# Row means of a 64 MB tensor: the first rows in parts of their own, and the last rows summed as two halves at once

## The chip, the cores and the metric

The kernel runs on one core of a Trainium2 chip. The metric is the device time of one execution in microseconds. Before the change it is 161.2 us, the median of 8 runs (161.05 to 161.87).

## The reference

```python
x = np.random.randn(32, 512, 1024).astype(np.float32)
divisor = 1024.0

def reference(x, divisor):
    return (np.sum(x, axis=-1) / divisor).astype(np.float32)
```

There are 32 x 512 = 16384 rows of 1024 floats (4 KB each, 67.1 MB in all). Each row is summed and multiplied by 1/1024. The output is 16384 floats, 64 KB.

## The kernel before

The 16384 rows are spread over the 128 partitions, 128 rows to each. They are cut into two parts in memory. The main part has M = 112 rows per partition: partition p holds rows 112p to 112p + 111, so that two neighbouring partitions read addresses 448 KB apart. The last part has L = 16 rows per partition, 64 KB apart, behind the main part.

The main part is loaded as tiles of 2, 14 (six times), 14 and 12 rows per partition, into a pool `bulk` of three buffers of 14 rows. The last part is loaded as 8, 4 and 2 rows, one whole row (`row`), and one row in three pieces of 448, 256 and 320 columns (`pa`, `pb`, `pc`). The 8-row tile takes a buffer of `bulk`; the rest have tiles of their own in the pool `one`. All loads are issued by SP in program order (line 142), and the loads of one core run through the same 16 DMA engines in that order. A load into a `bulk` buffer waits until DVE is done with the tile that was in it.

DVE sums rows with `reduce_sum` (line 153), all rows of a tile in one instruction. For the later tiles ACT takes some of the rows, one instruction for each row, which writes a copy to PSUM that nobody reads and the sum as its accumulator (line 147): 4 of 14, 5 of 12, 4 of 8, 2 of 4, 1 of 2. The sums of the main part go to `res`, which GpSimd scales once, after the last of them (line 189), and which SP then stores (line 190). The sums of the last part go to `q`. Of the whole row, DVE sums 768 columns into `q` (line 176) and ACT sums and scales 256 into `r`. At the end ACT sums `pa` and DVE sums `pb` (line 193), each into a spare column of `pc`; DVE makes `fin` from `q` and `r` (line 194), and then scales `pc` with its two spare columns and sums it, in one instruction with an accumulator (line 198), into the last column of `fin`. SP stores `fin` (line 201).

Three functions rearrange the finished program, and the change leaves them as they are. The first loads, which wait for nothing, are moved ahead of the start barrier. The waits of an instruction are sorted, so that the one expected last stands last. The last store is moved behind SP's waits for every other transfer and engine, and the closing barriers run while it is in flight; its own wait, for DVE, is kept on it. So SP issues the last store only after all earlier loads and stores have landed.

Of the kernel before, what the change touches and what calls it, by code (L numbers as in the profile page):

```python
# [8 lines left out]

F32 = mybir.dt.float32  # L10
ADD = mybir.AluOpType.add
MULT = mybir.AluOpType.mult
COPY = mybir.ActivationFunctionType.Copy
AX = mybir.AxisListType.X
SP = mybir.EngineType.SP
# [52 lines left out]
def close_while_storing(nc, landed):  # L68


    body, end = nc.main_func.blocks[1], nc.main_func.blocks[-1]
    store = [i for i in body.instructions if i.engine == SP and type(i).__name__ == "InstDMACopy"][-1]
    (lane,) = store.sync_info.on_update
    drain = end.instructions[0]
    assert drain.engine == SP and type(drain).__name__ == "InstDrain"
    needs = {w.id: w for w in drain.sync_info.on_wait}
    assert needs[lane.id].wait_value > lane.update_value
    needs[lane.id] = dataclasses.replace(
        needs[lane.id], wait_value=needs[lane.id].wait_value - lane.update_value
    )  # L80

    (done,) = [w for w in store.sync_info.on_wait if w.ant_name.startswith("DVE_")]
    assert needs[done.id].wait_value == done.wait_value
    del needs[done.id]
    own = dict(sync_type="semaphore", id=landed.num, ant_name=landed.name)
    add = mybir.SyncUpdate(update_mode="sem-add-imm", update_value=16, **own)
    sub = mybir.SyncUpdate(update_mode="sem-sub-imm", update_value=16, **own)
    last = nc.sync.wait_ge(landed, 16).ins
    assert nc.main_func.blocks[-1].instructions[-1].name == last.name
    body.instructions = [i for i in body.instructions if i.name != store.name]  # L90
    end.instructions = [
        with_sync(drain, on_wait=tuple(needs.values())),
        with_sync(store, on_wait=(done,), on_update=(add,)),
        *end.instructions[1:-1],
        with_sync(last, on_update=(sub,)),
    ]


@with_exitstack
def kernel(  # L100
    ctx: ExitStack,
    tc: tile.TileContext,
    x: bass.AP,
    divisor: float,
    out: bass.AP,
):
    nc = tc.nc
    landed = nc.alloc_semaphore("landed")
    nc.at_finalize(start_loads_at_once)
    nc.at_finalize(latest_wait_first)  # L110
    nc.at_finalize(lambda nc: close_while_storing(nc, landed))
    xf = x.flatten_outer_dims()
    N, D = xf.shape
    P = nc.NUM_PARTITIONS
    scale = 1.0 / float(divisor)
    J = N // P
    assert J * P == N


    L = 16  # L120
    M = J - L
    x_main = bass.AP(tensor=x.tensor, offset=0, ap=[[M * D, P], [D, M], [1, D]])
    x_last = bass.AP(tensor=x.tensor, offset=P * M * D, ap=[[L * D, P], [D, L], [1, D]])
    o_main = bass.AP(tensor=out.tensor, offset=0, ap=[[M, P], [1, M]])
    o_last = bass.AP(tensor=out.tensor, offset=P * M, ap=[[L, P], [1, L]])


    main = [(2, 0)] + [(14, 0)] * 6 + [(14, 4), (12, 5)]
    last = [(8, 4), (4, 2), (2, 1)]
    assert sum(n for n, _ in main) == M and sum(n for n, _ in last) == L - 2  # L130
    bulk = ctx.enter_context(tc.tile_pool(name="bulk", bufs=3))
    one = ctx.enter_context(tc.tile_pool(name="one", bufs=1))
    psum = ctx.enter_context(tc.tile_pool(name="junk", bufs=4, space=bass.MemoryType.PSUM))

    res = one.tile([P, M], F32, name="res")
    fin = one.tile([P, L], F32, name="fin")
    q = one.tile([P, L], F32, name="q")
    r = one.tile([P, L], F32, name="r")
    nc.gpsimd.memset(r, 0.0)  # L139

    def load(dst, src):
        tc.keep_in_program_order(nc.sync.dma_start(out=dst, in_=src))  # L142

    def act_sum(dst, src, by=1.0):
        n = src.shape[-1]
        junk = psum.tile([P, D], F32, name="junk")
        nc.scalar.activation(junk[:, :n], src, COPY, scale=by, accum_out=dst)  # L147

    def sums(dst, t, rows, on_act):
        d = rows - on_act  # L150
        for i in range(d, rows):
            act_sum(dst[:, i : i + 1], t[:, i, :])
        nc.vector.reduce_sum(out=dst[:, :d], in_=t[:, :d, :], axis=AX)  # L153

    j = 0
    for rows, on_act in main:
        t = bulk.tile([P, 14, D], F32, name="t")
        load(t[:, :rows, :], x_main[:, j : j + rows, :])
        sums(res[:, j : j + rows], t, rows, on_act)
        j += rows  # L160
    j = 0
    for rows, on_act in last:
        if rows == 8:
            t = bulk.tile([P, 14, D], F32, name="t")[:, :8, :]
        else:
            t = one.tile([P, rows, D], F32, name=f"t{rows}")
        load(t, x_last[:, j : j + rows, :])
        sums(q[:, j : j + rows], t, rows, on_act)
        j += rows


    c = 768
    row = one.tile([P, D], F32, name="row")
    load(row, x_last[:, j, :])
    act_sum(r[:, j : j + 1], row[:, c:], by=scale)
    nc.vector.reduce_sum(out=q[:, j : j + 1], in_=row[:, :c], axis=AX)  # L176

    a, b = 448, 704  # L180
    pa = one.tile([P, a], F32, name="pa")
    pb = one.tile([P, b - a], F32, name="pb")
    pc = one.tile([P, D - b + 2], F32, name="pc")
    load(pa, x_last[:, L - 1, :a])
    load(pb, x_last[:, L - 1, a:b])
    load(pc[:, : D - b], x_last[:, L - 1, b:])


    nc.gpsimd.tensor_scalar_mul(out=res, in0=res, scalar1=scale)  # L189
    tc.keep_in_program_order(nc.sync.dma_start(out=o_main, in_=res))  # L190

    act_sum(pc[:, D - b : D - b + 1], pa)
    nc.vector.reduce_sum(out=pc[:, D - b + 1 :], in_=pb, axis=AX)  # L193
    nc.vector.scalar_tensor_tensor(  # L194
        out=fin[:, : L - 1], in0=q[:, : L - 1], scalar=scale, in1=r[:, : L - 1], op0=MULT, op1=ADD
    )
    scaled = one.tile([P, D - b + 2], F32, name="scaled")
    nc.vector.tensor_scalar(  # L198
        out=scaled, in0=pc, scalar1=scale, scalar2=0.0, op0=MULT, op1=ADD, accum_out=fin[:, L - 1 :]
    )  # L200
    tc.keep_in_program_order(nc.sync.dma_start(out=o_last, in_=fin))


# [33 lines left out]
```

## Time and profile before

| | |
|---|---|
| median of 8 runs | 161.2 us |
| the profiled execution, its own time | 161.05 us |
| its span, first to last instruction | 159.5 us |
| DVE busy | 121.1 us (76%), 17 instructions |
| ACT busy | 19.6 us (12%), 37 instructions |
| POOL busy | 0.8 us |
| DMA, share of 16 engines over the span | 98.0% |
| read from HBM | 67.11 MB, 421 GB/s over the span |

The span is what the trace covers; 1.55 us of the profiled execution's time lie outside it. Times in the views are counted from the start of the span. Busy times of the engines overlap each other and the transfers. A DMA issue is shown with the time that SP spends on it, and separately with the time from issue to landing, which for a load that is queued behind others is mostly waiting in the queue.

### The profile page before, as it was taken

What the parts mean: (1) busy time and instruction counts of PE and PEld (TensorE: products, weight loads), DVE (VectorE), ACT (ScalarE), POOL (GpSimd) and SP (SyncE); (2) the same over time, 40 slices, a digit from 0 to 9 for tenths busy, and PEclk for the clock granted to TensorE, in tenths of its full rate; (3) what the DMA queues carried; (4) which work ended last, traced back from release to release, by engine and by line L of the source; (5) the groups of instructions that cost most, each with busy time, mean ns of one, the idle gap of its engine ahead of it and who ended that gap; (6) DMA issues with size and microseconds to landing.
All of it is one profiled execution on the core that took longest, in us unless ns stands there. A gap on an engine that the chain in (4) does not pass through costs nothing.

```text
span 159.5 us, 139 instructions
## 1 busy us (share of the span) xinstructions
DVE 121.1 (76%) x17; ACT 19.6 (12%) x37; POOL 0.8 (0%) x6
## 2 busy tenths in 40 slices
DVE  0500069995999599968999699959995996494985
ACT  3000000000000000000000000000001900480973
POOL 0000000000000000000000000000000000001000
DMA  9899999988999999987999999978999999899993
GB/s 349 374 460 460 460 460 460 460 388 360 403 460 460 460 460 460 460 374 345 431 460 460 460 460 460 460 331 360 460 460 427 394 493 493 345 444 386 413 400 132
DMA packets 2592, 67.18 MB, mean 421 GB/s; under 512 B 544, under 2 KB 928, under 8 KB 1056
## 3 DMA queue, kind: packets, MB, share of 16 engines
q1 hardware_dynamic: 2592, 67.18, 98.0%
HBM read 67.11 MB, written 0.07 MB: 421 GB/s over the span
## 4 chain that ended last, share of the span: by engine, by line
DMA 76%; DVE 22%; SPq 0%; issue 0%; DVEq 0%
DMA t<-in_x_dram 76%; DVE res L153 20%; DVE q L153 1%; DVE q L176 1%; SPq L142 0%; DVE scaled L198 0%; DVE pc L193 0%; DVE fin L194 0%; DVEq L198 0%; DVEq L232 0%
## 5 line engine op out<-in xcount | busy, mean ns | idle before, releaser
L153 DVE TENSOR_REDUCE res<-t 128x14 f32<-128x14336 f32 (+3 forms) x9 | 111.2, 12360 | 34.1 <-DMA t<-in_x_dram 34.1
L147 ACT ACTIVATE junk<-t 128x1024 f32<-128x1024 f32 x16 | 16.2, 1012 | 135.7 <-DMA t<-in_x_dram 135.7
L153 DVE TENSOR_REDUCE q<-t 128x4 f32<-128x4096 f32 (+2 forms) x3 | 7.9, 2642 | 2.7 <-DMA t<-in_x_dram 2.5
L147 ACT ACTIVATION_READ_ACCUMULATOR junk<-t 128x1 f32 x16 | 3.0, 186 | 0.0
L147 ACT ACT_TABLE_LOAD x1 | 1.3, 1283 | 1.7 <-PEq L218 1.7
L189 POOL TENSOR_SCALAR res<-res 128x112 f32<-128x112 f32 x1 | 0.5, 492 | 143.6 <-DVE res L153 143.6
L176 DVE TENSOR_REDUCE q<-row 128x1 f32<-128x768 f32 x1 | 1.0, 953 | 0.0
L198 DVE TENSOR_SCALAR_CACHE_REDUCE scaled<-pc 128x322 f32<-128x322 f32 x1 | 0.5, 489 | 0.1
L147 ACT ACTIVATE junk<-pa 128x448 f32<-128x448 f32 x1 | 0.5, 548 | 0.0
L193 DVE TENSOR_REDUCE pc<-pb 128x1 f32<-128x256 f32 x1 | 0.4, 412 | 0.0
L147 ACT ACTIVATE junk<-row 128x256 f32<-128x256 f32 x1 | 0.4, 387 | 0.1
L194 DVE SCALAR_TENSOR_TENSOR fin<-q,r 128x15 f32<-128x15 f32 x1 | 0.2, 174 | 0.0
L147 ACT ACTIVATION_READ_ACCUMULATOR junk<-row 128x1 f32 x1 | 0.2, 187 | 0.0
L147 ACT ACTIVATION_READ_ACCUMULATOR junk<-pa 128x1 f32 x1 | 0.2, 187 | 0.0
L139 POOL MEMSET r<- 128x16 f32 x1 | 0.1, 111 | 1.3 <-POOLq L218 1.3
L218 POOL MEMSET const-bfloat16-1.0<- 128x1 bf16 x1 | 0.1, 101 | 0.0
L218 POOL MEMSET const-uint8-127<- 128x1 uint8 x1 | 0.1, 101 | 0.0
L218 POOL MEMSET const-float32-0.0<- 128x1 f32 x1 | 0.1, 98 | 0.2 <-issue 0.2
L218 POOL MEMSET const-float32-1.0<- 128x1 f32 x1 | 0.1, 98 | 0.0
L198 DVE DVE_READ_ACCUMULATOR scaled<-pc 128x1 f32 x1 | 0.1, 83 | 0.0
## 6 DMA issues: line engine op xcount, KB each, us to landing
t<-in_x_dram SPq DMA_DIRECT2D x7, 7168.0 KB, 35.7
t<-in_x_dram SPq DMA_DIRECT2D x1, 6144.0 KB, 33.3
t<-in_x_dram SPq DMA_DIRECT2D x1, 4096.0 KB, 26.1
t<-in_x_dram SPq DMA_DIRECT2D x2, 1024.0 KB, 18.5
t<-in_x_dram SPq DMA_DIRECT2D x1, 2048.0 KB, 30.5
row<-in_x_dram SPq DMA_DIRECT2D x1, 512.0 KB, 33.2
pa<-in_x_dram SPq DMA_DIRECT2D x1, 224.0 KB, 33.3
pc<-in_x_dram SPq DMA_DIRECT2D x1, 160.0 KB, 33.0
```

What stands on the lines that cost most here:

```text
L139: nc.gpsimd.memset(r, 0.0)
L147: nc.scalar.activation(junk[:, :n], src, COPY, scale=by, accum_out=dst)
L153: nc.vector.reduce_sum(out=dst[:, :d], in_=t[:, :d, :], axis=AX)
L176: nc.vector.reduce_sum(out=q[:, j : j + 1], in_=row[:, :c], axis=AX)
L189: nc.gpsimd.tensor_scalar_mul(out=res, in0=res, scalar1=scale)
L193: nc.vector.reduce_sum(out=pc[:, D - b + 1 :], in_=pb, axis=AX)
L194: nc.vector.scalar_tensor_tensor(out=fin[:, : L - 1], in0=q[:, : L - 1], scalar=scale, in1=r[:, : L - 1], op0=MULT, op1=ADD)
L198: nc.vector.tensor_scalar(out=scaled, in0=pc, scalar1=scale, scalar2=0.0, op0=MULT, op1=ADD, accum_out=fin[:, L - 1 :])
L218: nc = _bacc.Bacc("TRN2", target_bir_lowering=False, num_devices=1)
```

## The change

The memory is cut differently. The first 2 rows of each partition (`head`) form a part of their own, 8 KB apart, so that it is one stretch of 1 MB. The next 14 rows (`first`) form another, 56 KB apart. The other 112 rows of each partition lie 448 KB apart; the first 96 of them are the main part, and the remaining 16 the last part. The tiles up to the last part keep their sizes (2, 14, then 14 five times, 14 and 12).

Each of the three parts ahead of the last one has its own result tile (`res_head`, `res_first`, `res`), scaled on GpSimd once its sums are there. The three are stored one after the other, behind all the loads in SP's queue.

The last part is loaded as 9, 4 and 2 rows and one row in two pieces of 576 and 448 columns (`pa`, `pb`). ACT takes the same numbers of rows as before (4, 2, 1), and now scales them itself. DVE no longer reduces these rows with one instruction for a tile. For each row it runs `tensor_tensor_reduce`, which adds the left half of the row to the right half, scales, writes the result over the left half, and has the sum of it as its accumulator; in the program each of these is followed by an instruction of its own that writes the accumulator to `fin`. `pa` is summed in this way into a spare column of `pb`, and then `pb`, with its two spare columns (the second of them zero), into the last column of `fin`. `row`, `pc`, `q`, `r` and `scaled`, and the instructions that combined them, are gone.

An unused tile of 224 floats is placed ahead of the others, and some tiles are allocated larger than they are used, so that every tile starts on a 64-byte boundary.

```diff
-    L = 16
-    M = J - L
-    x_main = bass.AP(tensor=x.tensor, offset=0, ap=[[M * D, P], [D, M], [1, D]])
-    x_last = bass.AP(tensor=x.tensor, offset=P * M * D, ap=[[L * D, P], [D, L], [1, D]])
...
-    main = [(2, 0)] + [(14, 0)] * 6 + [(14, 4), (12, 5)]
-    last = [(8, 4), (4, 2), (2, 1)]
+    E, F, L = 2, 14, 16
+    M = J - E - F - L
+
+    def part(row, pitch, n):
+        rows = bass.AP(tensor=x.tensor, offset=row * D, ap=[[pitch * D, P], [D, n], [1, D]])
+        return rows, bass.AP(tensor=out.tensor, offset=row, ap=[[pitch, P], [1, n]])
+
+    x_head, o_head = part(0, E, E)
+    x_first, o_first = part(P * E, F, F)
+    x_main, o_main = part(P * (E + F), M + L, M)
+    x_last, o_last = part(P * (E + F) + M, M + L, L)
+
+    head, first = [(E, 0)], [(F, 0)]
+    main = [(14, 0)] * 5 + [(14, 4), (12, 5)]
+    last = [(9, 4), (4, 2), (2, 1)]
...
+    pad = ctx.enter_context(tc.tile_pool(name="pad", bufs=1))
+    pad.tile([P, 224], F32, name="pad")
...
+    c = 576
+    t4 = one.tile([P, 4, D], F32, name="t4")
+    t2 = one.tile([P, 2, D], F32, name="t2")
+    pa = one.tile([P, 768], F32, name="pa")[:, :c]
+    pb = one.tile([P, D - c + 16], F32, name="pb")[:, : D - c + 2]
...
+    nc.gpsimd.memset(pb[:, D - c :], 0.0)
...
+    def dve_mean(dst, src, by=scale):
+        h = src.shape[-1] // 2
+        nc.vector.tensor_tensor_reduce(
+            out=src[:, :h], in0=src[:, :h], in1=src[:, h:], scale=by, scalar=0.0,
+            op0=ADD, op1=ADD, accum_out=dst,
+        )
+
+    parts = ((head, x_head, res_head), (first, x_first, res_first), (main, x_main, res))
+    for loads, src, dst in parts:
+        j = 0
+        for rows, on_act in loads:
...
+            nc.vector.reduce_sum(out=dst[:, j : j + d], in_=t[:, :d, :], axis=AX)
+            j += rows
+        nc.gpsimd.tensor_scalar_mul(out=dst, in0=dst, scalar1=scale)
     j = 0
     for rows, on_act in last:
...
         load(t, x_last[:, j : j + rows, :])
-        sums(q[:, j : j + rows], t, rows, on_act)
+        d = rows - on_act
+        for i in range(rows):
+            if i < d:
+                dve_mean(fin[:, j + i : j + i + 1], t[:, i, :])
+            else:
+                act_sum(fin[:, j + i : j + i + 1], t[:, i, :], by=scale)
         j += rows
-    c = 768
-    row = one.tile([P, D], F32, name="row")
-    load(row, x_last[:, j, :])
-    act_sum(r[:, j : j + 1], row[:, c:], by=scale)
-    nc.vector.reduce_sum(out=q[:, j : j + 1], in_=row[:, :c], axis=AX)
...
-    a, b = 448, 704
-    load(pa, x_last[:, L - 1, :a])
-    load(pb, x_last[:, L - 1, a:b])
-    load(pc[:, : D - b], x_last[:, L - 1, b:])
+    load(pa, x_last[:, j, :c])
+    load(pb[:, : D - c], x_last[:, j, c:])
...
-    nc.gpsimd.tensor_scalar_mul(out=res, in0=res, scalar1=scale)
+    tc.keep_in_program_order(nc.sync.dma_start(out=o_head, in_=res_head))
+    tc.keep_in_program_order(nc.sync.dma_start(out=o_first, in_=res_first))
     tc.keep_in_program_order(nc.sync.dma_start(out=o_main, in_=res))
...
-    act_sum(pc[:, D - b : D - b + 1], pa)
-    nc.vector.reduce_sum(out=pc[:, D - b + 1 :], in_=pb, axis=AX)
-    nc.vector.scalar_tensor_tensor(
-        out=fin[:, : L - 1], in0=q[:, : L - 1], scalar=scale, in1=r[:, : L - 1], op0=MULT, op1=ADD
-    )
-    nc.vector.tensor_scalar(
-        out=scaled, in0=pc, scalar1=scale, scalar2=0.0, op0=MULT, op1=ADD, accum_out=fin[:, L - 1 :]
-    )
+    dve_mean(pb[:, D - c : D - c + 1], pa, by=1.0)
+    dve_mean(fin[:, j:], pb)
     tc.keep_in_program_order(nc.sync.dma_start(out=o_last, in_=fin))
```

More of the change, by code (lines that the diff above doesn't have):

```diff
@@ L11 @@
 ADD = mybir.AluOpType.add
-MULT = mybir.AluOpType.mult
 COPY = mybir.ActivationFunctionType.Copy
@@ L117 @@
     assert J * P == N
-    L = 16
-    M = J - L
-    x_main = bass.AP(tensor=x.tensor, offset=0, ap=[[M * D, P], [D, M], [1, D]])
-    x_last = bass.AP(tensor=x.tensor, offset=P * M * D, ap=[[L * D, P], [D, L], [1, D]])
-    o_main = bass.AP(tensor=out.tensor, offset=0, ap=[[M, P], [1, M]])
-    o_last = bass.AP(tensor=out.tensor, offset=P * M, ap=[[L, P], [1, L]])
-    main = [(2, 0)] + [(14, 0)] * 6 + [(14, 4), (12, 5)]
-    last = [(8, 4), (4, 2), (2, 1)]
-    assert sum(n for n, _ in main) == M and sum(n for n, _ in last) == L - 2
+    E, F, L = 2, 14, 16
[10 more added lines that the diff above has]
+    last = [(9, 4), (4, 2), (2, 1)]
+    assert sum(n for n, _ in main) == M and sum(n for n, _ in last) == L - 1
+    pad = ctx.enter_context(tc.tile_pool(name="pad", bufs=1))
+    pad.tile([P, 224], F32, name="pad")
     bulk = ctx.enter_context(tc.tile_pool(name="bulk", bufs=3))
@@ L133 @@
     psum = ctx.enter_context(tc.tile_pool(name="junk", bufs=4, space=bass.MemoryType.PSUM))
+    c = 576
[3 more added lines that the diff above has]
+    pb = one.tile([P, D - c + 16], F32, name="pb")[:, : D - c + 2]
+    res_head = one.tile([P, 16], F32, name="res_head")[:, :E]
+    res_first = one.tile([P, 16], F32, name="res_first")[:, :F]
     res = one.tile([P, M], F32, name="res")
     fin = one.tile([P, L], F32, name="fin")
-    q = one.tile([P, L], F32, name="q")
-    r = one.tile([P, L], F32, name="r")
-    nc.gpsimd.memset(r, 0.0)
+    nc.gpsimd.memset(pb[:, D - c :], 0.0)
     def load(dst, src):
@@ L144, in act_sum @@
     def act_sum(dst, src, by=1.0):
-        n = src.shape[-1]
         junk = psum.tile([P, D], F32, name="junk")
[L147 to L160, printed above, removed]
+        nc.scalar.activation(junk, src, COPY, scale=by, accum_out=dst)
@@ new lines, in dve_mean @@
+    def dve_mean(dst, src, by=scale):
[8 more added lines that the diff above has]
+        for rows, on_act in loads:
+            t = bulk.tile([P, 14, D], F32, name="t")
+            load(t[:, :rows, :], src[:, j : j + rows, :])
+            d = rows - on_act
+            for i in range(d, rows):
+                act_sum(dst[:, j + i : j + i + 1], t[:, i, :])
+            nc.vector.reduce_sum(out=dst[:, j : j + d], in_=t[:, :d, :], axis=AX)
+            j += rows
+        nc.gpsimd.tensor_scalar_mul(out=dst, in0=dst, scalar1=scale)
@@ L161 @@
     j = 0
     for rows, on_act in last:
[L163 to L166, printed above, removed]
+        t = bulk.tile([P, 14, D], F32, name="t")[:, :rows, :] if rows > 4 else t4 if rows == 4 else t2
         load(t, x_last[:, j : j + rows, :])
-        sums(q[:, j : j + rows], t, rows, on_act)
-        j += rows
-    c = 768
-    row = one.tile([P, D], F32, name="row")
-    load(row, x_last[:, j, :])
@@ L175 @@
-    act_sum(r[:, j : j + 1], row[:, c:], by=scale)
-    nc.vector.reduce_sum(out=q[:, j : j + 1], in_=row[:, :c], axis=AX)
-    a, b = 448, 704
-    pa = one.tile([P, a], F32, name="pa")
-    pb = one.tile([P, b - a], F32, name="pb")
-    pc = one.tile([P, D - b + 2], F32, name="pc")
-    load(pa, x_last[:, L - 1, :a])
-    load(pb, x_last[:, L - 1, a:b])
-    load(pc[:, : D - b], x_last[:, L - 1, b:])
-    nc.gpsimd.tensor_scalar_mul(out=res, in0=res, scalar1=scale)
-    tc.keep_in_program_order(nc.sync.dma_start(out=o_main, in_=res))
@@ L192 @@
-    act_sum(pc[:, D - b : D - b + 1], pa)
-    nc.vector.reduce_sum(out=pc[:, D - b + 1 :], in_=pb, axis=AX)
-    nc.vector.scalar_tensor_tensor(
-        out=fin[:, : L - 1], in0=q[:, : L - 1], scalar=scale, in1=r[:, : L - 1], op0=MULT, op1=ADD
-    )
-    scaled = one.tile([P, D - b + 2], F32, name="scaled")
-    nc.vector.tensor_scalar(
-        out=scaled, in0=pc, scalar1=scale, scalar2=0.0, op0=MULT, op1=ADD, accum_out=fin[:, L - 1 :]
-    )
+        d = rows - on_act
+        for i in range(rows):
[3 more added lines that the diff above has]
+                act_sum(fin[:, j + i : j + i + 1], t[:, i, :], by=scale)
```

## The prediction

> **What bounds the kernel now.** I read the profile in this order: the page's chain, the timeline, the waits of SP's own queue, and the groups by form. The chain of waits shows the order of bounds:
>
> ```profile
> DMA 76%; DVE 22%; SPq 0%; issue 0%; DVEq 0%
> ```
>
> The 22% of DVE looks like a second bound, but the timeline takes it back:
>
> ```profile
> 21.51 15.09 DVE L153 TENSOR_REDUCE res<-t 128x14 f32<-128x14336 f32 x1 [14.61 <-DMA t<-in_x_dram]
> 38.47 15.09 DVE L153 TENSOR_REDUCE res<-t 128x14 f32<-128x14336 f32 x1 [1.87 <-DMA t<-in_x_dram]
> 55.41 15.09 DVE L153 TENSOR_REDUCE res<-t 128x14 f32<-128x14336 f32 x1 [1.86 <-DMA t<-in_x_dram]
> ```
>
> The columns are start, length and, in brackets, the idle time before it and what ended it. Each 14-row reduction starts 16.94 us after the last and takes 15.09, so DVE waits 1.86 us for every tile: the loads set the pace at 16.94 / 14 = 1.21 us per row of all partitions. DMA is busy 98.0% (the page's queue part). With three tiles and 1.86 us to spare, the loads never wait for DVE. So only three things count: how soon the stream starts, how many bytes and transfers it has, and what follows its last byte. The same view gives the end:
>
> ```profile
> 147.42 4.42 DVE L153 TENSOR_REDUCE q<-t 128x4 f32<-128x4096 f32 x1 [2.10 <-DMA t<-in_x_dram]
> ...
> 152.25 2.29 DVE L153 TENSOR_REDUCE q<-t 128x2 f32<-128x2048 f32 x1 [0.41 <-DMA t<-in_x_dram]
> ...
> 154.69 1.22 DVE L153 TENSOR_REDUCE q<-t 128x1 f32<-128x1024 f32 x1
> ...
> 155.93 0.95 DVE L176 TENSOR_REDUCE q<-row 128x1 f32<-128x768 f32 x1
> ...
> 157.00 0.41 DVE L193 TENSOR_REDUCE pc<-pb 128x1 f32<-128x256 f32 x1
> 157.53 0.49 DVE L198 TENSOR_SCALAR_CACHE_REDUCE scaled<-pc 128x322 f32<-128x322 f32 x1
> 157.94 0.08 DVE L198 DVE_READ_ACCUMULATOR scaled<-pc 128x1 f32 x1
> 158.05 0.34 SPq L201 DMA_DIRECT2D out_dram<-fin  x1
> ```
>
> The last load (pc) is issued at 124.17 and takes 33.0 us to land (issues part), so at 157.2. Then come the rest of line 193 (to 157.41), 0.12 us of waiting on DVE's own result, 0.49 for line 198, the store at 158.05, and 1.4 us until it lands: 159.5. About 0.85 us pass between the last landing and the last store. One more chain ends near there, in SP's own waits:
>
> ```profile
> SPq L232 <- DMA out_dram<-res: 0.6, 1, 0.6
> ...
> SPq L201 <- DVE scaled L198: 0.5, 1, 0.5
> ```
>
> SP may not issue the last store before the store of res has landed (issued 145.93, 11.5 us: at 157.4). Then it still waits 0.5 us for DVE. That 0.5 us is the cover under which the store of res lies.
>
> **What the Trainium skill says.** "Vector Engine (DVE) Microarchitecture Reference", section Measured stream behaviour on trn2: one- and two-source operations cost 1.0417 ns per column, plus about 75 ns per instruction when queued back to back, programs of several steps too. The trace agrees on the slope for one source: (15086 - 1220) / 13312 columns = 1.0416 ns, with a fixed part of 153 ns in the shown duration. It has two sources only in the 15-column operation of line 194 (174 ns), too short to tell the slope. The same page, section Points that are easy to get wrong, says an operation of that kind with two non-bf16 SBUF sources and an accumulator halves its throughput; no run here shows it, and it is my slow rival. "SBUF — State Buffer", section Who interferes with whom: two SBUF inputs on DVE contend with a GpSimd instruction that reads SBUF. In the trace the scaling of res runs from 145.41 to 145.90, while DVE idles until 147.42. "DMA: Bandwidth & Descriptors", section Latency and other measured facts: row pitches at large powers of two halve the rate. The trace shows 448 KB and 64 KB (the last part) both at 1.21 us per row; 8 and 56 KB it does not show.
>
> **The change part by part.**
>
> *Loads.* The bytes stay, and so do the 112 rows ahead of the last part. The loads fall from 16 to 14: row, pa, pb, pc (two rows) become one more row in the 8-row tile, and pa and pb. Row to pc took 157.2 - 154.67 = 2.54 us for two rows, 2.42 by the rate, so 0.03 us per small load. The new landings, from the old ones: 9 rows at 147.40 + 1.21 = 148.61; 4 rows 4.83 later, 153.44; 2 rows 2.44 later, 155.88; pa (576/1024 of a row, 0.68 + 0.03) 156.59; pb 157.15. The last byte comes 0.06 us earlier.
>
> *DVE in the last 16 rows.* A row costs 512 columns of a two-source operation instead of 1024 of a reduction. I take 153 + 533 = 0.69 us each, and nothing more for the accumulator read, since at line 198 the 83 ns read begins at 157.94 and ends with the operation that it follows. Bounds: 0.61 (the page's 75 ns) to 0.69 + 0.08 + 0.08 = 0.85 us (a read that nothing overlaps, and its own start). Five such rows after 148.61 end by 152.1 (at most 152.9), two after 153.44 by 154.9 (155.2), both before the next tile: the work is hidden. What is left: the one row of the 2-row tile, 155.90 to 156.60; pa (288 columns, 0.45 us) from 156.63 to 157.08; the wait on DVE's own result, 0.12 us as at line 198; pb (225 columns, 0.39, plus 0.02 for its odd split) from 157.20 to 157.61. The old end was 158.02, so DVE is done 0.41 us sooner. Lines 176, 193, 194 and 198 (0.95, 0.41, 0.17, 0.49) and ACT's two partial sums go. ACT's last row starts at 155.90 and is done at 157.05 (1.03, plus the rest of a 0.19 read), before DVE.
>
> *Stores and SP.* Scaling 2 and 14 columns on GpSimd stands beside one-input reductions: nothing. The three stores of head, first and res are issued after all loads, some 0.4 us each around 124 us and at 145.9, with nothing needed behind them: nothing. But two more stores of tiny rows (8 and 56 bytes) now lie in the DMA queue ahead of res. Store of res, last byte of pc to landing: 0.2 us; the two new ones cost between nothing and that each, and I take 0.1. So res lands at 157.15 + 0.2 + 0.2 = 157.55 instead of 157.42, and SP, which now also waits for ACT there (one more semaphore instruction, 0.05), was free at 157.5 and is free at 157.68. That is 0.07 us after DVE: the cover is gone, SP is late next, and the last store is issued at 157.68 instead of 158.05. If the tiny stores cost their upper bound, it is 157.88. The last store's rows now lie 448 bytes apart instead of side by side; I keep its 1.4 us, with 0.1 either way.
>
> *Start.* Rows 0 to 15 are read at 8 and 56 KB pitch. The first tile lands at 4.59 us; two rows at the rate are 2.42 and a whole small store takes 1.4 from issue to landing, so at most 0.77 us could be saved at the start. Nothing shows which way the new pitch goes. I take 0, bounds -0.3 to +0.5. Moved tile addresses: the stream already runs at 7168 KB / 16.94 us = 433 GB/s, steadily; 0.
>
> *Sum.* 158.05 - 157.68 = 0.37 us off the span: 159.5 to 159.13. The profiled run took 161.05 us, 1.55 more than its span, so 160.68 for its like; its median of 8 is 161.2, and 161.2 - 0.37 = 160.8.
>
> **The rivals.** A difference under 0.2%, 0.32 us here, is about what a measurement of this kernel can't tell from none.
>
> *The accumulator reads don't overlap.* Each of the last three operations costs 0.08 to 0.16 more, and DVE ends between 157.85 and 158.02. For it: the trace has one read, with nothing behind it. Against: it lies wholly inside its operation. Gain 0 to 0.2: 161.1.
>
> *The new operation runs at two cycles per column (the slower side).* Place: DVE after 148.61. 512 columns cost 153 + 1067 = 1.22 us; five rows end at 154.7, two at 157.2, one at 158.4, pa (0.75) at 159.15, pb (0.62 and 0.12) at 159.9, so the last store goes 1.9 us later: 163.1. It decides once an operation costs 0.13 us more than my price in each of the last three (0.41 / 3), and past 0.96 us per row even the five rows are late. For it: the page's sentence. Against: the same page's measured slope.
>
> *Stream or stores slower.* Head and first at their new pitches read more slowly (each per cent on 16 rows is 0.19 us), or the landing of 8-byte rows comes over 0.5 us late and holds SP's last store. It takes 0.7 us to turn the sign beyond doubt; I put it at 161.7. Against: two pitches in the trace ran alike.
>
> *The start gains.* Rows side by side begin sooner by 0.3 us: 160.5.
>
> **How the numbers follow.** Forecast 48% (own range 160.5 to 161.1: 32 points faster, 16 same), reads not overlapped 17% (2 faster, 12 same, 3 slower), two cycles 12% (slower), stream or stores 16% (15 slower, 1 same), start 7% (faster). Together faster 0.41, same 0.29, slower 0.30. The range 160.3 to 162.0 leaves out the two-cycle case and the far parts of the last two, under 2 in 10.
>
> **What would show it.** Right: 512-column operations near 0.69 us, starting at most 0.75 apart; pb's operation beginning near 157.2 right after pa's; the last store near 157.7, held by SP's wait for a store rather than by DVE. The first tile landing at 4.59 and tiles 16.94 us apart would confirm the stream. Wrong: operations of 1.2 us, or DVE still in the 9-row tile at 153.4; a first landing after 5 us; or a time outside the span that differs from 1.55 us.

## The result, and the profile after

The changed kernel takes 163.6 us (median of 11 runs, 162.89 to 164.41) against 161.23 us for the kernel before (32 runs). The ratio of the means is 1.0133, with a 95% interval of 1.0117 to 1.0149: slower by 1.3%, where the prediction said faster by 0.2%. The profiled execution took 163.63 us, its span is 162.1 us, so 1.5 us lie outside it, as before: the loss is inside the span.

The timeline of the changed kernel, in the stretch that answers to the one shown of before (start, length, engine and line, operation; in brackets the idle time before it):

```profile
148.79 0.69 DVE L167 CUSTOM_DVE_ANT_0 t<-t 128x512 f32<-128x512 f32 x1 [3.26 <-DMA t<-in_x_dram]
149.41 0.08 DVE L167 DVE_READ_ACCUMULATOR2_ANT fin<- 128x1 f32 x1
149.41 0.69 DVE L167 CUSTOM_DVE_ANT_0 t<-t 128x512 f32<-128x512 f32 x1
...
156.13 0.69 DVE L167 CUSTOM_DVE_ANT_0 t<-t 128x512 f32<-128x512 f32 x1 [1.12 <-DMA t<-in_x_dram]
156.75 0.08 DVE L167 DVE_READ_ACCUMULATOR2_ANT fin<- 128x1 f32 x1
156.84 0.46 DVE L167 CUSTOM_DVE_ANT_0 pa<-pa 128x288 f32<-128x288 f32 x1
157.22 0.08 DVE L167 DVE_READ_ACCUMULATOR2_ANT pb<- 128x1 f32 x1
157.45 0.40 DVE L167 CUSTOM_DVE_ANT_0 pb<-pb 128x225 f32<-128x225 f32 x1
157.77 0.08 DVE L167 DVE_READ_ACCUMULATOR2_ANT fin<- 128x1 f32 x1
160.65 0.33 SPq L205 DMA_DIRECT2D out_dram<-fin  x1
```

DVE is done at 157.85, earlier than the 158.02 of the kernel before. But the last store is issued at 160.65 instead of 158.05. For 2.8 us no engine works. The waits of SP's own queue (what was waited for, total, times, longest) name what SP stands at:

```profile
SPq L236 <- DMA out_dram<-res: 3.1, 1, 3.1
SPq L236 <- DMA pa<-in_x_dram: 0.7, 1, 0.7
...
SPq L236 <- DMA pb<-in_x_dram: 0.5, 1, 0.5
```

That wait was 0.6 us before. The DMA issues (size, and time from issue to landing) show the stores that lie in front of it:

```profile
pb<-in_x_dram SPq DMA_DIRECT2D x1, 224.0 KB, 33.9
out_dram<-res SPq DMA_DIRECT2D x1, 48.0 KB, 14.4
out_dram<-res_head SPq DMA_DIRECT2D x1, 1.0 KB, 35.7
out_dram<-res_first SPq DMA_DIRECT2D x1, 7.0 KB, 35.3
out_dram<-fin SPq DMA_DIRECT2D x1, 8.0 KB, 1.4
```

pb was issued at 123.44 and lands at 157.4. The store of res_head, 1 KB, was issued at 123.92 and lands at 159.6; res_first (124.48) at 159.8 and res (146.10) at 160.5. In the trace's records of the 16 DMA engines, the data packets of the res_head store start between 156.59 and 157.11 and take 9 ns each, but the 16 engines report it landed one after another, from 157.10 to 159.61. The 8 KB store of fin, 64-byte rows, has all its 16 reports within 0.16 us. So the bytes were sent before pb had landed, but the last report of their landing came 2.2 us after that of pb, which is ahead of them in the queue.

One more difference is at the start: the first tile is summed from 4.88 us instead of 4.62.

### The profile page after: what moved, and what is told of

Same layout as the page of the kernel before. It is cut to its first block, busy times and chain, and to the rows that moved or that the text cites. A ratio compares the mean times of both kernels' runs of the same rounds, so it can differ in the third digit from the quotient of the medians.

```text
span 162.1 us, 150 instructions
## 1 busy us (share of the span) xinstructions
DVE 117.3 (72%) x29; ACT 18.5 (11%) x33; POOL 1.2 (1%) x8
## 4 chain that ended last, share of the span: by engine, by line
DMA 76%; DVE 20%; SPq 1%; issue 0%; DVEq 0%
DMA t<-in_x_dram 55%; DMA pb<-in_x_dram 21%; DVE res L181 19%; DVE res_head L181 1%; SPq L157 1%; DVE pb L167 0%; DVEq L236 0%
## 5 line engine op out<-in xcount | busy, mean ns | idle before, releaser
L181 DVE TENSOR_REDUCE res<-t 128x14 f32<-128x14336 f32 (+2 forms) x7 | 93.9, 13409 | 14.8 <-DMA t<-in_x_dram 14.8
L181 DVE TENSOR_REDUCE res_first<-t 128x14 f32<-128x14336 f32 x1 | 15.1, 15086 | 14.7 <-DMA t<-in_x_dram 14.7
L167 DVE CUSTOM_DVE_ANT_0 t<-t 128x512 f32<-128x512 f32 x8 | 5.1, 690 | 6.1 <-DMA t<-in_x_dram 6.1
L181 DVE TENSOR_REDUCE res_head<-t 128x2 f32<-128x2048 f32 x1 | 2.3, 2286 | 4.9 <-DMA t<-in_x_dram 4.9
L183 POOL TENSOR_SCALAR res<-res 128x96 f32<-128x96 f32 x1 | 0.5, 457 | 108.4 <-DVE res L181 108.4
L167 DVE DVE_READ_ACCUMULATOR2_ANT fin<- 128x1 f32 x9 | 0.7, 83 | 0.0
L167 DVE CUSTOM_DVE_ANT_0 pa<-pa 128x288 f32<-128x288 f32 x1 | 0.5, 458 | 0.0
## 6 DMA issues: line engine op xcount, KB each, us to landing
pa<-in_x_dram SPq DMA_DIRECT2D x1, 288.0 KB, 33.9
pb<-in_x_dram SPq DMA_DIRECT2D x1, 224.0 KB, 33.9
```

The lines of the kernel that those rows point to most:

```text
L167: nc.vector.tensor_tensor_reduce(out=src[:, :h], in0=src[:, :h], in1=src[:, h:], scale=by, scalar=0.0, op0=ADD, op1=ADD, accum_out=dst,)
L181: nc.vector.reduce_sum(out=dst[:, j : j + d], in_=t[:, :d, :], axis=AX)
L183: nc.gpsimd.tensor_scalar_mul(out=dst, in0=dst, scalar1=scale)
```

## The experiments

Theory: one of the two new stores of tiny rows lands late, and since SP issues the last store only after every other transfer has landed, it moves the end. Rivals: the number of stores, the store of res itself, the new way of summing, and a slower stream of loads.

**1 to 3: leave the small stores out, one at a time and both.**

```diff
 # run e1 leaves out the first line, e2 the second, e3 both
-    tc.keep_in_program_order(nc.sync.dma_start(out=o_head, in_=res_head))
-    tc.keep_in_program_order(nc.sync.dma_start(out=o_first, in_=res_first))
     tc.keep_in_program_order(nc.sync.dma_start(out=o_main, in_=res))
```

> The changed kernel without the store of the first 2 columns (8-byte rows); those outputs are left out. Theory A (the 8-byte rows land late and hold SP's last store): the store of the 14 columns and that of res land within 0.5 us of their last byte, the last store is issued near 158.0, span about 159.4. Theory B (the 56-byte rows are what lands late): the last store stays near 160.5, span about 162. Theory C (it is the number of stores, about 0.9 us each): the last store near 159.7, span about 161.2.

> The changed kernel without the store of the next 14 columns (56-byte rows); those outputs are left out. Theory A (8-byte rows late): the last store stays near 160.4, span about 161.9. Theory B (56-byte rows late): the last store near 158.0, span about 159.4. Theory C (number of stores): the last store near 159.7, span about 161.2.

> The changed kernel without both small stores; those outputs are left out. All three theories on the stores: DVE ends near 157.8, SP is not held, the last store is issued before 158.0, span about 159.4, time about 160.9, some 0.3 us under the kernel before. Rival D (the store of res itself, or the wait for ACT, is what holds SP): the last store stays after 159, span above 160.5.

Without the 8-byte rows: 161.28 us, ratio 0.9999 (0.9987 to 1.001), span 159.6. Without the 56-byte rows: 164.22 us (two runs), ratio 1.0179 (1.0151 to 1.0206), span 162.7. Without both: 160.85 us, ratio 0.9971 (0.9961 to 0.9981), span 159.2. The last store and SP's wait ahead of it, first without the 8-byte rows:

```profile
158.18 0.33 SPq L204 DMA_DIRECT2D out_dram<-fin  x1
```

```profile
SPq L235 <- DMA out_dram<-res_first: 0.3, 1, 0.3
```

Without the 56-byte rows:

```profile
161.29 0.33 SPq L204 DMA_DIRECT2D out_dram<-fin  x1
```

```profile
SPq L235 <- DMA out_dram<-res_head: 3.2, 1, 3.2
```

Without both small stores:

```profile
157.61 0.08 DVE L167 DVE_READ_ACCUMULATOR2_ANT fin<- 128x1 f32 x1
157.72 0.34 SPq L203 DMA_DIRECT2D out_dram<-fin  x1
```

```profile
SPq L234 <- DMA out_dram<-res: 0.2, 1, 0.2
```

Here the last store is issued 0.03 us after DVE's last instruction ends, and SP's wait for the store of res is 0.2 us. Together the three runs bear out theory A: the 8-byte rows cost the time, and all of the loss goes with the two stores. Without the 56-byte rows the last store comes even later than theory A had it (161.29 against 160.4). A price for each store is refuted by the second run, which has one store fewer and is not faster. The store of res and the wait for ACT, which the third run keeps, hold nothing. The 56-byte rows are not free either: with them alone SP's last store is at 158.18 instead of 157.72, of which 0.29 us is a later landing of pb in that execution.

**4: issue the small stores early,** between loads, so that their landing lies beside the stream.

```diff
             load(t[:, :rows, :], src[:, j : j + rows, :])
+            if src is x_main and j == 14:
+                tc.keep_in_program_order(nc.sync.dma_start(out=o_head, in_=res_head))
+            if src is x_main and j == 28:
+                tc.keep_in_program_order(nc.sync.dma_start(out=o_first, in_=res_first))
...
-    tc.keep_in_program_order(nc.sync.dma_start(out=o_head, in_=res_head))
-    tc.keep_in_program_order(nc.sync.dma_start(out=o_first, in_=res_first))
```

> The changed kernel, with the two small stores issued by SP among the loads, right after the loads of the fourth and the fifth tile, instead of behind all loads; nothing left out. If the small stores' late landing is all that the change loses, it is hidden here: the last store is issued near 157.9, span about 159.4, time about 160.9, ratio to the kernel before 0.998. Rival: small rows in the middle of the stream slow the loads behind them; then tiles come later than 16.94 us apart and the time stays above 161.3.

It takes 163.66 us, ratio 1.0141 (1.0117 to 1.0164): nothing gained, and the rival of that expectation is right. The timeline of DVE around the place of the small stores:

```profile
38.66 15.09 DVE L185 TENSOR_REDUCE res<-t 128x14 f32<-128x14336 f32 x1 [1.85 <-DMA t<-in_x_dram]
55.66 15.09 DVE L185 TENSOR_REDUCE res<-t 128x14 f32<-128x14336 f32 x1 [1.91 <-DMA t<-in_x_dram]
75.07 15.09 DVE L185 TENSOR_REDUCE res<-t 128x14 f32<-128x14336 f32 x1 [4.33 <-DMA t<-in_x_dram]
91.89 15.09 DVE L185 TENSOR_REDUCE res<-t 128x14 f32<-128x14336 f32 x1 [1.74 <-DMA t<-in_x_dram]
```

Tiles come 17.0 us apart, then once 19.41, then 16.8. The 16 engines report the res_head store between 55.48 and 58.26, and the load behind it, which SP had issued at 36.83, is late by 2.4 us. By the trace's records of packets, a 56 KB packet of a load takes 2.12 to 2.14 us in the stream ahead of this store; behind it, of the 26 that start between 55.0 and 57.5, 18 take longer, up to 4.45. So the 8-byte rows do not only land late: they hold the DMA engines, and what is queued behind them on the engines waits. The loss moves into the stream, which is the bound of this kernel, so the store costs as much here as at the end of the queue. The 56-byte rows, sent between 73.8 and 74.6, do not hold it: the packets around them take 2.12 us, and the next tile comes 16.8 us after the last.

**5 and 6: the two halves of the change, each alone.** The first keeps the memory as it was cut before and changes the last 16 rows; the second keeps the old sums and changes the cut and its three stores.

```diff
 # e5: the changed kernel with the old cut
-    E, F, L = 2, 14, 16
-    M = J - E - F - L
+    L = 16
+    M = J - L
... (the parts, their results and their two small stores go as well)
 # e6: the kernel before, with the new parts and their stores
-    L = 16
-    M = J - L
+    E, F, L = 2, 14, 16
+    M = J - E - F - L
... (the parts, their results and their three stores come in)
```

> The change to the last rows alone (9, 4, 2 rows, two pieces of the last row, halves summed at once, wait for ACT at the end), with the memory cut as in the kernel before and so no small stores. By the prediction's steps without its store term: DVE ends near 157.6, last store at 157.65 to 157.75, span 159.1, time about 160.85, ratio 0.9975 (first tile at 4.6). If the new cut of memory also costs at the start, as the one profile of the changed kernel suggests (first tile at 4.85), this beats the kernel without small stores (160.85) by 0.2 to 0.3: about 160.6.

> The new cut of memory alone, with its three stores, and the last 16 rows summed as in the kernel before. If the 8-byte rows hold SP whatever DVE does: the last store is issued near 160.6 and the time is 163 to 164.5, as slow as the whole change or slower by no more than 0.3, because the landing and not DVE sets the end. Rival: the new way of summing is part of the loss; then this is clearly faster than the changed kernel, under 162.5.

The sums alone take 160.9 us, ratio 0.9974 (0.9965 to 0.9984): a gain of 0.37 us of 161.27, near the 0.41 by which the prediction had DVE done sooner. (The profiled execution is the slowest of the nine, and its last load lands at 157.62, so the gain shows in what follows: from the last landing to the last store pass 0.54 us, against 0.83 before.) The 160.6 us that the expectation had, if the new cut also costs at the start, did not come. The cut alone takes 164.03 us (two runs), ratio 1.0163 (1.0142 to 1.0185), span 162.7. In its trace DVE is done at 158.44 and SP still stands at the store of res:

```profile
158.36 0.08 DVE L211 DVE_READ_ACCUMULATOR scaled<-pc 128x1 f32 x1
161.26 0.33 SPq L214 DMA_DIRECT2D out_dram<-fin  x1
```

```profile
SPq L245 <- DMA out_dram<-res: 4.7, 1, 4.7
```

So the loss belongs to the cut and the gain to the sums. In the whole change the gain lies hidden behind the wait: DVE is done 2.8 us before the last store.

**7 and 8: what makes the rows slow.** One part of 16 rows instead of parts of 2 and 14. Its result is stored in one piece (64-byte rows side by side), or in two pieces of 2 and 14 columns: the same 8-byte rows as in the change, but 64 bytes apart.

```diff
-    x_head, o_head = part(0, E, E)
-    x_first, o_first = part(P * E, F, F)
+    x_first, o_first = part(0, E + F, E + F)
...
-    head, first = [(E, 0)], [(F, 0)]
+    first = [(E, 0), (F, 0)]
...
 # run 7 keeps the one store of o_first; run 8 has in its place:
+    tc.keep_in_program_order(nc.sync.dma_start(out=o_first[:, :E], in_=res_first[:, :E]))
+    tc.keep_in_program_order(nc.sync.dma_start(out=o_first[:, E:], in_=res_first[:, E:]))
```

> The changed kernel with its first 16 rows in one part (64 KB apart), so one store of 64-byte rows side by side instead of the two of 8 and 56 bytes; nothing left out. If it is rows shorter than 64 bytes (or not on 64-byte borders) that land late: this store lands within 0.5 us of its last byte, the last store is issued before 158.0, time 160.8 to 161.1. Rival (any store of a small area, with many rows close together, is slow): the landing stays over 1 us late, time above 162.

> As the kernel with one 16-row part, but its result is stored in two pieces: 2 columns (8-byte rows, now 64 bytes apart, each in a 64-byte piece of its own) and 14 columns (56-byte rows, 64 apart). If 8-byte rows are slow because several of them fall into the same 64 bytes and have to wait for each other: both land within 0.7 us of their last byte, last store before 158.3, time under 161.4. If a row shorter than 64 bytes is slow by itself: landing about 2.5 us late, time 163 or more.

With one store of 64-byte rows: 160.76 us, ratio 0.9966 (0.9952 to 0.9979), nothing left out: it beats both kernels. Its last store:

```profile
157.67 0.33 SPq L202 DMA_DIRECT2D out_dram<-fin  x1
```

With 8-byte rows 64 bytes apart: 161.22 us, ratio 1.0004 (0.9989 to 1.0018). The issues of the latter:

```profile
pb<-in_x_dram SPq DMA_DIRECT2D x1, 224.0 KB, 33.9
out_dram<-res SPq DMA_DIRECT2D x1, 48.0 KB, 11.9
out_dram<-res_first SPq DMA_DIRECT2D x1, 1.0 KB, 33.7
out_dram<-res_first SPq DMA_DIRECT2D x1, 7.0 KB, 33.5
```

The same 1 KB in the same 128 rows of 8 bytes lands 33.7 us after its issue here, and 35.7 in the change, with pb taking 33.9 in both. So 8 bytes is not too short by itself; the distance of the rows decides.

**9 to 11: how many rows share 64 bytes.** Parts of 4 and 12 rows (16-byte rows, four to 64 bytes, and 48-byte rows), of 8 and 8 (32-byte rows), and of 8 and 8 with the first result stored as 2 and 6 columns.

```diff
-    E, F, L = 2, 14, 16
 # run 9:
+    E, F, L = 4, 12, 16
 # runs 10 and 11:
+    E, F, L = 8, 8, 16
...
 # run 11 besides:
-    tc.keep_in_program_order(nc.sync.dma_start(out=o_head, in_=res_head))
+    tc.keep_in_program_order(nc.sync.dma_start(out=o_head[:, :2], in_=res_head[:, :2]))
+    tc.keep_in_program_order(nc.sync.dma_start(out=o_head[:, 2:], in_=res_head[:, 2:]))
```

> The changed kernel with parts of 4 and 12 rows: the first store has 16-byte rows side by side (four in each 64 bytes), the second 48-byte rows. Theory M1 (rows that fall into the same 64 bytes are written one after the other, some 0.35 us each: 2.5 us for eight): landing of the first store some 1.1 us after its last byte, last store near 158.8, time near 162.0. Theory M2 (the rows of a small area are written one by one, some 0.02 us each whatever their size, because they go to one place of the memory): landing 2.5 us late, time 163.5 or more. Theory M3 (only 8-byte rows are slow): landing under 0.5 us late, time 161.3.

> The changed kernel with parts of 8 and 8 rows: both small stores have 32-byte rows side by side (two in each 64 bytes). M1: landing some 0.4 to 0.7 us after the last byte, last store near 158.1, time near 161.3. M2: each of the two lands 2.5 us late, together up to 5 us, time 163.5 to 166. M3: time 161.0 to 161.3.

> As the kernel with parts of 8 and 8 rows, but the first result is stored in 2 columns (8-byte rows, 32 bytes apart, two in each 64 bytes) and 6 columns (24-byte rows). M1: what counts is rows per 64 bytes, two as before: last store near 158.3 to 158.6, time 161.5 to 161.8. M2: 2.5 us for each of the three small stores, time above 164. M3 (8-byte rows slow whatever lies between them): already spoken against by the run with 64 bytes between them; here it would give 163.5.

They take 161.87 us (ratio 1.0029, 1.0016 to 1.0042), 161.09 us (0.9987, 0.9977 to 0.9996) and 162.44 us (1.0074, 1.0055 to 1.0092). Below, by the records of landings in one trace each, how much later the store of res, the last of the queue, lands than the last load:

| small stores, and row pieces written into each 64 bytes of the first | res lands after the last load, us | time, us |
|---|---|---|
| none (both left out) | 0.24 | 160.85 |
| 64-byte rows, 1 | 0.33 | 160.76 |
| 32-byte rows twice, 2 | 0.50 | 161.09 |
| 56-byte rows alone, 2 | 0.56 | 161.28 |
| 8 + 56 bytes in the same 64, 2 | 0.68 | 161.22 |
| 16- and 48-byte rows, 4 | 0.99 | 161.87 |
| 8 + 24 bytes in the same 32, 4, and 32-byte rows | 1.81 | 162.44 |
| 8- and 56-byte rows, 8 | 3.10 | 163.6 |
| 8-byte rows alone, 8 | 3.90 | 164.22 |

Part of this is the mere number of stores. With 64- and with 32-byte rows each store lands 0.16 to 0.17 us after the one ahead of it, so three stores make 0.5 us with no other cost. Over that, two pieces in the same 64 bytes cost nothing to 0.2 us, four 0.5 to 1.1, eight 2.6 to 3.6. So the delay grows with the number of pieces. The last two rows of the table are not shown to differ: the times without the 56-byte rows (164.18 and 164.26) lie within those of the changed kernel (162.89 to 164.41).

M2, a fixed price for every row of a small area, is refuted by the 32-byte rows: two such stores cost 0.3 us and not 2.5 each. M3, that only 8-byte rows are slow, is refuted by the eleventh run: there the 8-byte rows landed at 157.50, 0.26 after pb, and it is the 24-byte rows right behind them, into the same 64 bytes, that landed at 158.73.

M1 gave the times of the 16- and 32-byte rows to within 0.25 us, but not for its own reason in the first of them: the 16-byte rows landed 0.31 us after pb, where M1 had 1.1, and the delay showed at the store of res, 0.52 after the store ahead of it; besides, all loads of that execution came late, pb at 157.72 against 157.46 with 32-byte rows. The eleventh run was slower than M1 said (162.44 against at most 161.8). If the count takes in both stores that are in flight together, it has four pieces and not two. Even then it is no straight line: the four pieces of the 16-byte rows cost about half of that.

That 64 bytes is the unit is not shown either. Counted in pieces of 128 or 256 bytes the rows stand in much the same order. What the runs show is that short rows lying close together in memory are slow, 8 bytes apart most of all, and that 64-byte rows side by side are not.

What makes such writes wait for each other is not settled. "DMA: Bandwidth & Descriptors" of the Trainium skill, section Specifications, says that below 512 bytes a DMA engine reads, modifies and writes. The stores of 448-, 384- and 64-byte rows here landed 0.2 to 0.33 us after the last load, so length under 512 bytes is not by itself what costs microseconds. Nor was it tried whether it matters if one DMA engine or several write into the same 64 bytes.

## Why the prediction was wrong

*What bounds the kernel:* right. The stream sets the pace, and what ends last behind it, DVE's sums or the store of res, sets the rest.

*Loads:* right. From the landing of the 9-row tile at 148.77 to that of pb at 157.37 pass 8.60 us, where the working had 157.15 - 148.61 = 8.54.

*DVE:* right, with the rows a little too dear. The shape of 512 columns takes 0.69 us, as taken, 288 columns 0.46, 225 columns 0.40. The accumulator reads overlap not only with their own operation but with the next one, which starts with them: rows follow each other at 0.61 us (148.79, 149.41), the lower bound given, and the trace agrees here with the 75 ns per queued instruction of the Trainium skill's "Vector Engine (DVE) Microarchitecture Reference", section Measured stream behaviour on trn2 (533 + 75 = 608 ns). DVE is done 0.48 us after pb has landed; the prediction had 0.46. The rivals of reads that don't overlap and of two cycles per column both fall. The sentence behind the second, in that page's section Points that are easy to get wrong, names one instruction layout, `S2S2D2_STT`; the trace calls the new operation CUSTOM_DVE_ANT_0, so that it is "of that kind", as the prediction had it, is not shown, and the runs do not test the sentence.

*Start:* the new pitch was taken at 0. The first tile begins to be summed between 4.79 and 4.96 us in the six kernels whose first tile is read 8 KB apart, and between 4.50 and 4.62 in the four that read it 64 or 448 KB apart, some 0.3 us earlier. That lies inside the bounds given (-0.3 to +0.5), but no run shows that the end moves with it: the sums alone, at the old pitch, take 160.9 us, and the changed kernel without its small stores, at the new one, 160.85.

*Stores and SP:* this is the step that failed, in one term. The mechanism was there: the cover of 0.5 us is gone, and SP's wait for the stores is late next. The term "the two new ones cost between nothing and that each, and I take 0.1", where "that" is 0.2 us, was sized by the store of res, whose cost in the trace of before is 0.2 us for 448-byte rows that start 448 bytes apart. It stood at 0.2 for both and measured about 2.9 (3.10 less the 0.24 with both left out). The price was read from the nearest row by number of bytes, and the bytes are not what is paid for: 1 KB cost over ten times what the 48 KB behind it cost alone. The upper bound was a guess of the same kind, since no store in that trace puts more than one row into 64 bytes.

*The rivals:* the third one had this very place, the landing of 8-byte rows that holds SP's last store, and the point from which it decides, over 0.5 us late. It got 16% and a time of 161.7, which was 1.9 us short. In the prediction it stood together with a slower read of the first rows, where it should have had a bound of its own.

*The sum:* with 2.9 in place of 0.2 for the stores, and pb landed at 157.37 instead of 157.15, the last store comes at 157.68 + 2.7 + 0.22 = 160.60; it was measured at 160.65. Both sizes are read from the same trace, so this says only that no other term is missing.

## What to carry to other kernels

When a result is stored in parts, look at the distance between its rows in memory before you look at its bytes: 128 rows of 8 bytes side by side held the DMA engines here for 2 to 4 us, rows of 32 bytes cost next to nothing, and moving the slow store ahead didn't hide it, since the stream behind it is the bound. A part of 16 floats per partition (64-byte rows) had all of the gain and none of the loss. And where a wait covers all earlier transfers, give each new one a bound of its own, from a row of its own shape; if the trace has none, that is a wide unknown and not a small one.

## What the runs showed of the hardware that was not expected

- 128 rows of 8 bytes side by side (1 KB) took the 16 DMA engines from 157.10 to 159.61 us to report as landed; the same rows 64 bytes apart from 156.94 to 157.53, and 64-byte rows side by side from 156.75 to 157.29.
- The engines were held meanwhile: in the middle of the stream the same store made the next tile 2.4 us late, and 56 KB packets behind it took up to 4.45 us instead of 2.12.
- On DVE the instruction that reads the accumulator starts together with the next operation: 0.69 us each, 0.61 us from start to start.
- A first tile read 8 KB apart starts its sums about 0.3 us later than one read 64 or 448 KB apart (six traces against four); no run shows the difference at the end.
